# Encoder layer with a mixture of 32 experts: 32 extra rows for each of the 17 largest experts

## The chip, the cores and the metric

The kernel runs on one core of a Trainium2 chip. The metric is the device time of one execution in microseconds (us), taken as the median of several runs. The kernel before takes 2105.02 us (three runs, 2104.12 to 2105.26).

The engines that matter here are TensorE (PE for its products, PEld for its weight loads), VectorE (DVE), ScalarE (ACT), GpSimd (POOL) and the DMA engines, whose large loads are issued from SyncE's queue (SP).

## The reference

One layer over 1024 tokens of width 1024: a mixer (short convolution and Fourier group), a cross attention to 256 memory tokens, and a mixture of experts, which is most of the time:

```
logits = (hf @ w_router) + b_router                 # 1024 tokens, 32 experts
top_v, top_i = top_k(logits, 4)                     # 4 experts for each token
top_w = softmax(top_v)
for each expert e, for the rows (tokens) that chose it:
    gu   = xb @ w_gate_up[e] + b_gate_up[e]         # 1024 -> 2 x 1024
    gate = min(gu[:, :1024], 7); up = clip(gu[:, 1024:], -7, 7)
    out  = ((up + 1) * gate * sigmoid(1.702 * gate)) @ w_down[e] + b_down[e]
y = sum over the four experts of a token of out * weight
```

1024 tokens with four choices each make 4096 rows, 128 for an expert on average. How many rows an expert has depends on the inputs. The reference's inputs are drawn from seed 0 where nothing else is asked.

## The kernel before

Everything is float32. The weights of an expert are 12 chunks of 1 MB (`raw`): eight for gate and up, four for down. A chunk is loaded by SP's queue (line 973), ACT copies it into a rounded part `eh` (line 134), DVE takes the rest `el` (line 135), and PE makes three products for each 128 rows of contraction (lines 1062 to 1064). So a chunk costs PE 12 products, whatever rows the expert really has: the rows are always a block of 128.

The 32 experts are worked through one after another. Expert 0 is a "static" one, handled before the counts are known; the other 31 are sorted by how many rows they have, and the program speaks of ranks: rank 0 is the expert with most rows. Which weights a rank means is read from a table at run time; everything else is fixed when the program is built.

Rows of an expert beyond its first 128 have three ways:

- `rem_rows(r)` gives rank r a fixed number of further rows, 64, 32 or 0. Ranks with some are called heavy here, the others light. For a heavy expert `plan` puts further steps among the steps of the first 128 rows: `x_rem` gathers and transposes the rows (line 1035), six calls of `rem_mm` multiply them by the raw chunks in float32 (line 1085, eight products each, `j` = 1, 3, 5, 7, 9, 11), `take_rem` and `h_rem` make the hidden values (lines 1103 to 1125), and `y_rem` adds the result to memory (lines 1140 to 1145). The first of the six calls and `x_rem` stand in the last chunks of the expert ahead.
- `rem_mm` uses the width of TensorE: with 64 rows two products with different rows of the output run side by side, with 32 rows four do (`n = 64 // m`).
- What no rank's fixed rows hold goes to `beyond`, a loop near the end (line 1402) over blocks of 128 rows, as many as the counts ask for (`nblk`), none if they all fit. `_tables` gives it the room of each rank in `eid[:, 3] = [P + rem_rows(r) for r in e]`.

`rank_order` mixes heavy and light ranks so that they alternate as far as their numbers allow. The kernel before has 18 heavy ranks (two with 64 rows, 16 with 32) and 13 light ones. Its order after the static expert begins with ranks 0, 1, 18, 2, 19, 3, 4, 20, 5, 21, 6, 22, 7, 8. Two heavy experts stand next to each other in five places.

Within an expert, what is done after which half chunk is set by tables of numbers for each kind of expert (`PLACE_*`, `AHEAD_*`, `REM`): they say how many chunks ahead ACT and DVE split. Raw chunks and split pairs share 20 buffers of 8 KB per partition, so a load starts when a buffer comes free. The tables are chosen by kind (heavy, light, first, loop, last) and not by rank. All engines' work is in the order in which the program writes it.

Of the kernel before, what the change touches and what calls it, by code (L numbers as in the profile page):

```python
# [29 lines left out]
ALPHA = 1.702  # L30
N64 = 2
N32 = 18
STATIC = NE - 1
# [46 lines left out]
def kernel(ctx: ExitStack, tc: tile.TileContext, A, out, dbg=None):  # L80
# [39 lines left out]
    def rsqrt(dst, v, tmp):  # L120
        """1 / sqrt of positive columns times RS: a first guess from the exponent, three Newton steps, each without its last factor"""
        nc.vector.tensor_scalar(tmp.bitcast(I32), v.bitcast(I32), 1, None, op0=ALU.logical_shift_right)  # L122
        nc.vector.tensor_scalar(dst.bitcast(I32), tmp.bitcast(I32), -1.0, float(0x5F3759DF), op0=ALU.mult, op1=ALU.add)
        for c in (3.0, 12.0, 768.0):
            if v.shape[-1] == 1:
                nc.vector.scalar_tensor_tensor(tmp, dst, v, dst, op0=ALU.mult, op1=ALU.mult)
            else:
                nc.vector.tensor_tensor(tmp, dst, dst, op=ALU.mult)
                nc.vector.tensor_tensor(tmp, tmp, v, op=ALU.mult)
            nc.vector.scalar_tensor_tensor(dst, tmp, -c, dst, op0=ALU.add, op1=ALU.mult)  # L130
# [20 lines left out]
    def sum_cols(srcs):  # L151
        """sums over the partitions, a token on each partition, 128 tokens for each column; among the products that follow"""
        b = sm_bank("colps")
        k = 0
        for src in srcs:
            for j in range(src.shape[-1] // P):
                def one(k=k, s=src[:, j * P:(j + 1) * P]):
                    nc.tensor.matmul(b[:, k:k + 1], s, ones[:, 0:1], start=True, stop=True)
                fill.append(one)
                k += 1  # L160
        return b[:, :k]

    def rms_cols(b, width, eps_scale=1.0):
        """sums of squares to 1 / rms"""
        while fill:
            fill.pop(0)()
        c = small("rc", [P, 3, 16], bufs=2)
        v, y, t = (c[:, i, :b.shape[-1]] for i in range(3))
        nc.vector.tensor_scalar(v, b, eps_scale / width, eps_scale * EPS, op0=ALU.mult, op1=ALU.add)
        nc.scalar.activation(y, v, AF.Sqrt)  # L170
        nc.vector.reciprocal(y, y)
        nc.vector.tensor_tensor(t, y, y, op=ALU.mult)
        nc.vector.tensor_tensor(t, t, v, op=ALU.mult)
        nc.vector.tensor_scalar(t, t, -0.5, 1.5, op0=ALU.mult, op1=ALU.add)
        nc.vector.tensor_tensor(y, y, t, op=ALU.mult)
        return y
# [8 lines left out]
    def rms_row(dg, dst):  # L185
        """on every partition, a token in each column"""
        ps = sm_bank("rowps")[:, :dg.shape[-1]]
        nc.tensor.matmul(ps, ones, dg, start=True, stop=True)
        nc.scalar.activation(dst, ps, AF.Copy)
# [16 lines left out]

    # weights in their order of use: raw ahead, split one ahead
    specs = [(A["w_in"][12 + c], KT) for c in range(4)]
# [42 lines left out]

    # ---------------------------------------------------------------- constants
    vec = cp.tile([P, 52], F32, name="vec")
# [32 lines left out]

    # ------------------------------------------------------------ x^T and the Fourier group's projection
    xh = [[s8(f"xh{h}{g}", [P, 4, H2], F32R) for g in range(2)] for h in range(2)]
# [73 lines left out]

    # Fourier group: fold over n <-> N - n and n <-> N/2 - n, channel transform
    AB = []
# [43 lines left out]

    # short convolution group
    ych, ycl = [], []  # L410
# [96 lines left out]

    # ------------------------------------------------------------ sequence transform, memory side
    yfh = [s8(f"yfh{q}", [P, 2, S], F32R) for q in range(2)]
# [13 lines left out]
    def seq_out(ct, sb):  # L523
        """in three parts"""
        pq = []
# [80 lines left out]

    # ------------------------------------------------------------ output projection and first residual
    x1h = [[s8(f"x1h{h}{g}", [P, 4, H2], F32R) for g in range(2)] for h in range(2)]
# [39 lines left out]

    # ------------------------------------------------------------ attention over the memory
    # scale of the logits: rms / sqrt(head dim), one column for each token tile  # L650
    sc = []
# [86 lines left out]

    # v W_o for each head, then the second residual
    VW = []  # L740
# [19 lines left out]
    def row_table():  # L760
        """table of expert rows, all padding"""
        ptab = s8("ptab", [P, NE * ESTR // P, 2], I32)
        nc.gpsimd.iota(ptab[:, :, 0], pattern=[[1, NE * ESTR // P]], base=0, channel_multiplier=NE * ESTR // P)
        nc.vector.memset(f(ptab[:, :, 1]), 0.0)
        nc.vector.tensor_scalar(ptab[:, :, 0], ptab[:, :, 0], P - 1, None, op0=ALU.bitwise_and)
        nc.scalar.dma_start(out=tab_d.rearrange("(p j) c -> p j c", p=P), in_=ptab)
# [12 lines left out]
    def load_bias():  # L779
        """leading parts twice, then the rests: products with leading part, rest, leading part of the weights"""  # L780
        bd.extend([s4("bdn", [3 * NE, D], F32R), s4("bdr", [3 * NE, D])])
        for i in range(3):
            nc.scalar.dma_start(out=bd[1][i * NE:(i + 1) * NE], in_=A["b_down"])
# [10 lines left out]

    # ------------------------------------------------------------ router, one tile of 128 tokens at a time
    scat = []
# [4 lines left out]
    def tile_r(x2):  # L801
        """logits of two tiles, an expert on each partition, in four parts"""
        ps = lt["ps"] = sm_bank("lgps")
        for k in range(2):
            for g in range(4):
                nc.tensor.matmul(ps[g * NE:(g + 1) * NE, :HF], wr[:, 2 * g + k, :], x2(2 * g + k), start=k == 0, stop=k == 1)
        sb = lt["sb"] = t2("lgt")[:, :HF]
        nc.scalar.activation(sb, ps[:, :HF], AF.Copy)
# [106 lines left out]

    # ------------------------------------------------------------ experts
    order = rank_order()
# [59 lines left out]
    def whole(q):  # L977
        """chunks that are multiplied in float32 itself, where the tensor engine has the time"""
        return q < WHOLE_FIRST or q >= NE * 12 - WHOLE_LAST
# [90 lines left out]
    def rem_mm(i, j):  # L1070
        """rows 128.. of the pair of chunks j - 1, j: products for different rows of PSUM run side by side"""
        s = st[i]
# [32 lines left out]
    def h_rem(i, c):  # L1105
        """hidden values with the columns on the partitions; each sum has two parts"""
        s = st[i]
# [39 lines left out]
    def expert(i, hook=None, last=False):  # L1147
        """a chunk at a time; what else there is to do has its place after the first half of a chunk or after the chunk"""
        s = st[i]
# [49 lines left out]
    def plan(i):  # L1199
        """rows 128.. of an expert: some chunks ahead of the first 128, so that raw chunks are not held for them"""  # L1200
        lead, lx, lt, l0, l1, ly = REM
# [14 lines left out]

    # ------------------------------------------------------------ second residual, chunk by chunk
    def early():
        """positions of the static expert: rows of the first tiles within its first 128, the others beyond"""
        ps = sm_bank("exps")  # L1220
# [7 lines left out]
    def bias_load():  # L1228
        """gate biases on the first half of the partitions, up biases on the second: a leading part and the rest of each expert"""
        BT.extend([s4("BT", [P, D], F32R), s8("braw", [P, D])])  # L1230
# [26 lines left out]
    def places(*todo):  # L1257
        """what is done after each part of a chunk"""
        return {k: (lambda fs=fs: [fn(*arg) for fn, *arg in fs]) for k, fs in enumerate(todo)}
# [45 lines left out]
    def count_order():  # L1305
# [31 lines left out]
        def surplus():  # L1337
            """blocks of 128 rows beyond the rows that a rank has"""
            ps3[0] = sm_bank("ovps")
# [59 lines left out]
    def beyond():  # L1399
        """rows beyond: any number of blocks of 128"""  # L1400
        ordered.close()
# [52 lines left out]

    # ------------------------------------------------------------ last norm; the last expert's rows once more
    z = NE - 1
# [96 lines left out]
def _cols(w, n):  # L1553
    """[K, F] -> [F / n, P, K / P, n]"""
    return w.reshape(w.shape[0] // P, P, w.shape[1] // n, n).transpose(2, 1, 0, 3)


def _heads(w):
    """[4 * 256, D] -> [head, half of D, P, 2, 512]"""
    return w.reshape(4, 2, P, 2, H2).transpose(0, 3, 2, 1, 4)  # L1560
# [45 lines left out]
```

## Time and profile before

| what | value |
|---|---|
| median of three runs | 2105.02 us |
| span of the profiled execution, first to last instruction | 2097.7 us |
| around the span (median less span) | 7.3 us |
| stages before the experts | 0 to 620.8 us |
| expert 0 (static) | 620.8 to 696.5 us |
| experts 1 to 30 | 696.5 to 2041.0 us |
| last expert and final norm | 2041.0 to 2097.7 us |

The page gives the profiled execution a span and no time of its own; the 7.3 us are the difference from the median of the runs. An expert is taken to begin where PE starts the product with its bias row (line 1049), its first product. In the views below a row of the timeline is start, duration, engine, line, operation, output and inputs; a group row is line, engine, operation, shapes and count, then busy us, mean ns of one, and the engine's idle time before. Matmuls overlap in their durations, so the cost of a step on PE is read from the start of one row to the start of the next. One float32 product stands as two records, and one call of `rem_mm` as a row of x16.

### The profile page before, as it was taken

What the parts mean: (1) busy time and instruction counts of PE and PEld (TensorE: products, weight loads), DVE (VectorE), ACT (ScalarE), POOL (GpSimd) and SP (SyncE); (2) the same over time, 40 slices, a digit from 0 to 9 for tenths busy, and PEclk for the clock granted to TensorE, in tenths of its full rate; (3) what the DMA queues carried; (4) which work ended last, traced back from release to release, by engine and by line L of the source; (5) the groups of instructions that cost most, each with busy time, mean ns of one, the idle gap of its engine ahead of it and who ended that gap; (6) DMA issues with size and microseconds to landing.
All of it is one profiled execution on the core that took longest, in us unless ns stands there. A gap on an engine that the chain in (4) does not pass through costs nothing. (4 is left out here: it accounts for less than half of the span.)

```text
span 2097.7 us, 28863 instructions
## 1 busy us (share of the span) xinstructions
PE 2059.9 (98%) x10857; PEld 1521.2 (73%) x10857; DVE 1590.7 (76%) x2000; ACT 1124.9 (54%) x1200; POOL 233.0 (11%) x192
## 2 busy tenths in 40 slices
PE   8999999999989999999999999999999999999996
PEld 7888988888974567676777676767667767676764
DVE  6666778445666667888888897888888888888886
ACT  5233533344223455676566665667656567566764
POOL 0000100000232111011101011102111101110101
PEclk9999999999999999999999999999999999999998
DMA  4121434013266769897989887988798989798986
GB/s 156 50 65 61 146 120 157 21 41 124 94 245 252 249 224 327 296 327 267 340 309 366 300 318 272 343 304 325 278 331 313 356 296 320 273 344 306 341 303 241
DMA packets 105327, 514.06 MB, mean 245 GB/s; under 512 B 21697, under 2 KB 26050, under 8 KB 56034
## 3 DMA queue, kind: packets, MB, share of 16 engines
q1 hardware_dynamic: 83968, 445.88, 56.3%
q0 software_dynamic: 14400, 49.33, 9.6%
q10 hardware_dynamic: 6818, 16.99, 2.2%
q8 instruction: 86, 1.41, 0.3%
q14 instruction: 55, 0.45, 0.1%
HBM read 473.81 MB, written 38.34 MB: 244 GB/s over the span
## 5 line engine op out<-in xcount | busy, mean ns | idle before, releaser
L135 DVE TENSOR_TENSOR el<-raw,eh 128x2048 fp32r<-128x2048 f32 x372 | 831.3, 2287 | 134.6 <-ACT eh L134 133.1
L134 ACT ACTIVATE eh<-raw 128x2048 fp32r<-128x2048 f32 x372 | 690.5, 1908 | 7.2 <-PEq L1402 4.6
L1062 PE MATMUL g<-eh,xthl 128*128 128x512 f32 x992 | 401.3, 405 | 0.0
L1063 PE MATMUL g<-el,xthl 128*128 128x512 f32 x992 | 388.5, 392 | 2.0 <-DVE el L135 2.0
L1064 PE MATMUL g<-eh,xthl 128*128 128x512 f32 x992 | 388.2, 391 | 2.2 <-issue 2.2
L1062 PEld LDWEIGHTS g<-eh,xthl 128*128 128x128 f32 x992 | 186.5, 188 | 80.8 <-issue 42.6
L1064 PEld LDWEIGHTS g<-eh,xthl 128*128 128x128 f32 x992 | 186.6, 188 | 43.5 <-issue 2.6
L1063 PEld LDWEIGHTS g<-el,xthl 128*128 128x128 f32 x992 | 186.8, 188 | 37.9 <-DVE el L135 2.7
L1062 PE MATMUL d<-eh,hthl 128*128 128x512 f32 x496 | 205.9, 415 | 0.0
L1064 PE MATMUL d<-eh,hthl 128*128 128x512 f32 x496 | 195.0, 393 | 0.0
L1063 PE MATMUL d<-el,hthl 128*128 128x512 f32 x496 | 193.9, 391 | 0.0
L1085 PE MATMUL r<-raw,xrt 128*32 128x512 f32 (+1 forms) x1216 | 166.3, 598 | 0.7 <-ACT xrt L1036 0.7
L1001 ACT ACTIVATE sg<-g 128x512 f32<-128x512 f32 x64 | 40.4, 631 | 171.1 <-DVE g L1000 171.1
L940 POOL DMA_INDIRECT acc_d<-y,idx x31 | 78.2, 2522 | 384.7 <-ACT y L1131 302.4
L1062 PEld LDWEIGHTS d<-eh,hthl 128*128 128x128 f32 x496 | 93.2, 188 | 27.2 <-ACT xthl L134 9.2
L1064 PEld LDWEIGHTS d<-eh,hthl 128*128 128x128 f32 x496 | 93.1, 188 | 21.2
L1063 PEld LDWEIGHTS d<-el,hthl 128*128 128x128 f32 x496 | 93.6, 189 | 16.0
L1085 PEld LDWEIGHTS r<-raw,xrt 128*32 128x32 f32 (+1 forms) x1216 | 39.8, 113 | 87.0 <-issue 85.8
L134 ACT ACTIVATE hthl<-tp 128x512 fp32r<-128x512 f32 x62 | 37.1, 599 | 119.4 <-PE tp L1009 119.4
L145 PE MATMUL mm<-xh,wh 128*128 128x512 f32 x232 | 92.4, 398 | 5.8 <-ACT xh L137 5.8
L147 PE MATMUL mm<-xh,wl 128*128 128x512 f32 x232 | 91.2, 393 | 0.3 <-DVE wl L135 0.3
L146 PE MATMUL mm<-xl,wh 128*128 128x512 f32 x232 | 91.2, 393 | 0.0
(377 smaller groups left out, 3297.7 us busy)
## 6 DMA issues: line engine op xcount, KB each, us to landing
raw<-in_w_exp SPq DMA_DIRECT2D x375, 1024.0 KB
raw<-in_w_exp POOLq DMA_DIRECT2D x9, 1024.0 KB
wraw<-in_w_in SPq DMA_DIRECT2D x15, 512.0 KB
xraw<-in_xT SPq DMA_DIRECT2D x16, 256.0 KB
wraw<-in_w_k SPq DMA_DIRECT2D x8, 512.0 KB
wraw<-in_w_v SPq DMA_DIRECT2D x8, 512.0 KB
wraw<-in_w_out SPq DMA_DIRECT2D x8, 512.0 KB
xres<-in_xT SPq DMA_DIRECT2D x16, 256.0 KB
```

What stands on the lines that cost most here:

```text
L134: nc.scalar.activation(dh, src, AF.Copy)
L135: nc.vector.tensor_tensor(dl, src, f(dh), op=ALU.subtract)
L145: nc.tensor.matmul(ps, lh, rh, start=start and i == 0, stop=False)
L146: nc.tensor.matmul(ps, lh, rl, start=False, stop=False)
L147: nc.tensor.matmul(ps, ll, rh, start=False, stop=stop and i == n - 1)
L940: nc.gpsimd.indirect_dma_start(out=dst, out_offset=bass.IndirectOffsetOnAxis(ap=idx, axis=0), in_=src, in_offset=None, compute_op=ALU.add)
L1001: nc.scalar.activation(sg[:m, :n], g[:m, :n], AF.Sigmoid, scale=ALPHA)
L1062: nc.tensor.matmul(ps, l[:, 0, kk, :], wh[:, k, :], start=j >= 8 and g == 0 and k == 0, stop=False)
L1063: nc.tensor.matmul(ps, l[:, 0, kk, :], wl[:, k, :], start=False, stop=False)
L1064: nc.tensor.matmul(ps, l[:, 1, kk, :], wh[:, k, :], start=False, stop=g == 1 and k == 3)
L1085: nc.tensor.matmul(ps[o:o + m], lhs[:, g * 4 + kk, :], ch[12 * i + j - 1 + t][0][:, kk, :], start=k == 0 and g == 0, stop=k == 4 // n - 1 ...
```

## The change

Two numbers change: no rank has 64 further rows, and 17 ranks instead of 18 have 32.

```
-N64 = 2
-N32 = 18
+N64 = 0
+N32 = 17
 STATIC = NE - 1
```

The other lines of the diff take out comments and docstrings. `rem_rows` thus gives ranks 0 and 1 the number 32, ranks 2 to 16 stay at 32, and rank 17 goes from 32 to 0. The static expert keeps 64. Through `_tables` the loop is told of the smaller room. `rank_order` now has 17 heavy and 14 light ranks: 0, 1, 17, 2, 18, 3, 19, 4, 20, 5, 6, 21, 7, 22. Two heavy ones stand next to each other in three places.

PE at the end of expert 0, just ahead of expert 1's first product (`rd` is a part of expert 0, `r` the first `rem_mm` of expert 1, the two `g` rows its bias):

```order
 L1064 MATMUL d_6126<-eh,hthl 128x512
 L1085 MATMUL rd<-raw,hrt 64x512 x8
-L1085 MATMUL r_6236<-raw,xrt 64x512 x8
+L1085 MATMUL r_6236<-raw,xrt 32x512 x8
 L1049 MATMUL g_6261<-BT,ohr 128x512
 L1049 MATMUL g_6263<-BT,ohr 128x512
```

The number of products stays, eight, and each now makes 32 rows; nothing around them moves.

POOL, from the gathers for expert 5 on (`xg` are the 128 rows of the next expert, `xgr` its further rows, `acc_d<-yr` and `acc_d<-y` the results of the expert that ends); before:

```order
L936 DMA xg<-h_d,idx 128x1024
L936 DMA xgr<-h_d,idr 32x1024
L940 DMA acc_d<-y,idx 1152x1024
L936 DMA xg<-h_d,idx 128x1024
L936 DMA xgr<-h_d,idr 32x1024
L940 DMA acc_d<-yr,ids 2304x512
L940 DMA acc_d<-y,idx 1152x1024
L936 DMA xg<-h_d,idx 128x1024
L940 DMA acc_d<-yr,ids 2304x512
L940 DMA acc_d<-y,idx 1152x1024
```

And now:

```order
L936 DMA xg<-h_d,idx 128x1024
L936 DMA xgr<-h_d,idr 32x1024
L940 DMA acc_d<-y,idx 1152x1024
L936 DMA xg<-h_d,idx 128x1024
L940 DMA acc_d<-yr,ids 2304x512
L940 DMA acc_d<-y,idx 1152x1024
L936 DMA xg<-h_d,idx 128x1024
L936 DMA xgr<-h_d,idr 32x1024
L940 DMA acc_d<-y,idx 1152x1024
```

Where two heavy experts followed each other a light one now stands between them; the same moves are made on PE, DVE and ACT. Taken expert by expert, the rows of PE, DVE and ACT from expert 3 to the end are, in both programs, made of the same few sequences (heavy before light, heavy before heavy, light before heavy, and the last ones); only how often each stands there differs.

## Rows read from the trace of the kernel before

**Rows 1.** The page, part 1: busy time, share of the span, instructions.

```profile
PE 2059.9 (98%) x10857; PEld 1521.2 (73%) x10857; DVE 1590.7 (76%) x2000; ACT 1124.9 (54%) x1200; POOL 233.0 (11%) x192
```

**Rows 2.** Busy time by windows, experts 1 to 30; first its columns.

```profile
core 0: us, PE busy (x) PEld busy (x) DVE busy (x) ACT busy (x) POOL busy (x), PEclk, DMA share, GB/s
696.45:2040.95 1344.50, 1342.35 (x6914) 935.76 (x6912) 1114.54 (x982) 851.70 (x722) 167.10 (x95) 1.00 0.85 310
```

**Rows 3.** Waits of PE from 696 to 2041 us: total, times, longest.

```profile
PE g L1064 <- issue: 2.2, 1, 2.2
```

**Rows 4.** The same view by experts 1, 2, 6, 7, 8 and 30.

```profile
696.45:756.35 59.90, 59.90 (x278) 36.33 (x276) 42.95 (x38) 32.64 (x28) 6.36 (x4) 1.00 0.67 222
756.35:812.04 55.69, 55.69 (x256) 34.71 (x254) 35.12 (x34) 25.47 (x24) 5.71 (x3) 1.00 0.80 280
936.33:985.84 49.51, 49.51 (x280) 32.51 (x276) 40.95 (x41) 31.54 (x28) 6.64 (x4) 1.00 0.70 242
985.84:1032.95 47.11, 47.11 (x256) 31.52 (x252) 36.86 (x37) 27.33 (x25) 7.48 (x3) 1.00 0.94 344
1032.95:1071.55 38.60, 38.60 (x190) 29.72 (x189) 34.47 (x26) 27.20 (x24) 4.69 (x4) 1.00 0.93 347
1991.42:2040.95 49.53, 47.38 (x256) 31.43 (x252) 40.36 (x38) 29.05 (x25) 5.46 (x3) 1.00 0.79 297
```

**Rows 5.** Timeline of PE: one `rem_mm` with 64 rows, one with 32.

```profile
692.91 3.60 PE L1085 MATMUL r<-raw,xrt 128*64 128x512 f32 x16
696.45 0.50 PE L1049 MATMUL g<-BT,ohr 64*128 64x512 f32 x2
...
848.77 1.92 PE L1085 MATMUL r<-raw,xrt 128*32 128x512 f32 x16
850.62 0.50 PE L1049 MATMUL g<-BT,ohr 64*128 64x512 f32 x2
```

**Rows 6.** Timeline of DVE and PE, end of the light experts 8 and 12.

```profile
1063.60 4.50 DVE L135 TENSOR_TENSOR el<-raw,eh 128x2048 fp32r<-128x2048 f32 x2 [1.11 <-ACT eh L134]
...
1067.09 0.39 PE L1063 MATMUL d<-el,hthl 128*128 128x512 f32 x1
...
1235.01 4.50 DVE L135 TENSOR_TENSOR el<-raw,eh 128x2048 fp32r<-128x2048 f32 x2 [1.11 <-ACT eh L134]
...
1238.50 0.39 PE L1063 MATMUL d<-el,hthl 128*128 128x512 f32 x1
```

**Rows 7.** Groups of DVE by shape, experts 1 to 30, further rows only.

```profile
L1116 DVE TENSOR_TENSOR re<-tp,bT 128x256 f32<-128x256 f32 x32 | 13.5, 422 | 8.3 <-PE tp L1113 8.3
L1118 DVE TENSOR_TENSOR re<-re,tp 128x256 f32<-128x256 f32 x32 | 13.5, 421 | 1.1
L1141 DVE TENSOR_TENSOR yr<-rd,yr 64x512 f32<-64x512 f32 x16 | 10.8, 675 | 0.0
L1125 DVE SCALAR_TENSOR_TENSOR hrt<-ga 128x128 f32<-128x128 f32 x32 | 9.4, 294 | 1.1
L1124 DVE TENSOR_TENSOR ga<-ga 128x128 f32<-128x128 f32 x32 | 9.4, 293 | 7.9 <-ACT ga L1122 7.9
L1121 DVE TENSOR_SCALAR ga<-re 128x128 f32<-128x128 f32 x32 | 7.3, 227 | 1.1
L1123 DVE TENSOR_SCALAR ga<-re 128x128 f32<-128x128 f32 x32 | 7.0, 220 | 0.0
```

**Rows 8.** The loop's branches (line 1402), and one chunk multiplied in float32.

```profile
L1402 PEldq COMPARE_BRANCH  x3: 101/187/327, 1997.6 to 2002.0; - x3
...
630.89 3.60 PE L1054 MATMUL g<-raw,xthl 128*128 128x512 f32 x8
```

## The prediction

> **What bounds the kernel now.** I read the page's first part first: PE is busy for 98% of the span [rows 1]. That alone does not prove a bound, since matmul records overlap. So I cut the span into stages and looked at the stretch that the change touches, experts 1 to 30: of 1344.50 us PE has 1342.35 busy, at the granted clock 1.00, its upper level of 2.4 GHz [rows 2], and the waits of PE there are one, of 2.2 us, at the loop [rows 3]. DVE and the DMA engines are well used too (1114.54 us, and a share of 0.85) [rows 2], but PE never waits for them. Then I cut the stretch expert by expert at the bias products. Four kinds of windows come out: heavy before heavy 49.51 us, heavy before light 47.11, light before heavy 38.60, and the two experts with 64 rows, 59.90 and 55.69 [rows 4]. The trace has four windows of the first kind, eleven of the second and twelve of the third, and within a kind they agree to 0.03 us. A window that long and that constant, with PE busy in all of it, is the sum of its products. So time here is the number of PE products times their pace, and what the change does to that number is what it does to the time, as long as the others keep up.
>
> **The price of 32 rows.** Call the work that every expert has b, the part of a heavy expert's further rows that lies in the expert ahead X, and the part in its own window Y. Then b + X + Y = 49.51, b + Y = 47.11 and b + X = 38.60 [rows 4], so X = 49.51 - 47.11 = 2.40, Y = 49.51 - 38.60 = 10.91, b = 36.20. Being heavy with 32 rows costs X + Y = 13.31 us. As a check from below: one `rem_mm` takes from 848.77 to 850.62, 1.85 us [rows 5], and six make 11.1; the other 2.2 us are the small transposes around them.
>
> **The price of 64 rows.** Expert 1 has its own Y64 and expert 2's X64 in its window, expert 2 only its Y64. So Y64 = 55.69 - 36.20 = 19.49, X64 = 59.90 - 55.69 = 4.21, together 23.70 us [rows 4]. Check: one call takes from 692.91 to 696.45, 3.54 us against 1.85 [rows 5], close to double, since two products run side by side instead of four; six calls differ by 10.1 us, and the windows say 23.70 - 13.31 = 10.39.
>
> **What the change does, summed.** Ranks 0 and 1 go from 64 to 32: 2 x 10.39 = 20.8 us of PE. Rank 17 goes from heavy to light: 13.3 us. Together 34.1 us, all of it on PE, where nothing is idle. The order moves too, and this I cost at nothing, since X and Y are paid for each heavy expert wherever it stands. Counted in windows, experts 1 to 30 then have 3 x 49.51 + 14 x 47.11 + 13 x 38.60 + 2.4 for the loop's entry (the last heavy window is 49.53 instead of 47.11 [rows 4]) = 1312.3 against 1344.5 us, 32.2 less, and X64 - X = 1.8 us more goes from the static expert's window: 34.0. The rest of the span, the six last experts with their kinds and the final norm included, has the same work in the same order. Span: 2097.7 - 34.1 = 2063.6 us; with the 7.3 us that the median has beyond the span, **2070.9 us**, 1.6% less.
>
> **What hides what is left.** DVE's and ACT's work per expert hardly changes, but they get 34 us less for it. The cover: in the light-heavy rhythm the last chunk of a light expert is the tightest. In expert 8 the first of two `el` of 4.50 us together ends near 1065.9 and its first product starts at 1067.09, 1.2 us later; two rounds on, in expert 12, near 1237.3 and 1238.50, again 1.2 us [rows 6]. The margin is thin, but it is reset by each heavy expert and doesn't shrink from round to round. The change lengthens the unbroken rounds (the longest from three light experts before the next heavy pair to five), and nothing in the trace drifts with their length. Were that cover gone, a light expert would end later by what DVE lacks. The other place is new: expert 1 with 32 rows straight after the static one. Its window shrinks from 59.90 to 49.51 us with some 42 us of DVE work (42.95 before; 40.95 in another such window) [rows 4]; it fits, with 6.6 us to spare where that other window has 8.6, but the split of its chunks is entered from another state than anywhere in the trace. I bound what that costs between 0 and the 2.0 us by which its slack is smaller. I take 0, since windows with the same rows have no wait.
>
> **A page that says otherwise.** The PE row by itself, 98% [rows 1], is the reason for the sum. The Trainium skill, "Perfetto Trace Analysis", section "Identifying the Most-Contended Engine", holds that matmul busy time doesn't measure how near TensorE is to its limit, and wants the weight loads' share beside it; by that, DVE with 76% stands ahead of PEld with 73% [rows 1], and the change would be worth what it takes from DVE. The rows on PE's waits speak against reading it so here [rows 3]; it is the second rival.
>
> **Rivals.**
>
> *The loop runs (slower).* With zero blocks the loop is some branches: three on PE's queue of at most 0.33 us [rows 8], and no row of its body. The smaller room sends rows there as soon as a rank of 0 or 1 has over 160, or rank 17 over 128; that is the point from which it decides. Routing the reference's inputs of seed 0 through its own router gives ranks 0 to 3 the counts 154, 153, 150, 147, rank 16 130 and rank 17 126. So all fit, with six and two rows to spare, and the loop stays empty. This hangs on the draw: of seeds 1 to 8, seven have one to three ranks over 160. If a block ran, it would cost 12 chunks in float32 at 3.60 us [rows 8], 43 us, were the loads hidden; at 347 GB/s [rows 4] a chunk of 1.05 MB takes 3.0 us, and with loads and products in turn, since a product's two buffers are taken again by the next, 79 us. I take 79, as the loop has nothing else to overlap. 2070.9 + 79 = **2150 us** (2114 at least), and more with more blocks. Against it speak the counts; for it, only that the measured inputs could be drawn otherwise.
>
> *DVE or the loads are the bound (faster, little).* Then only DVE's part goes. A heavy expert has two of each of six groups, 2 x (422 + 421 + 227 + 220 + 293 + 294) ns = 3.75 us, and one of 675 ns [rows 7]: 4.4 us for rank 17, and next to nothing for ranks 0 and 1, which swap wide for narrow ones. 2105.0 - 4.4 = **2100.6 us**, just beyond 0.2%. Against it: PE would have to show waits for DVE now, and has none [rows 3].
>
> *Part of it comes back as stalls.* The thin 1.2 us per light expert [rows 6] turns into a wait, in each of 14 light experts, with at most that size: 2070.9 + 14 x 1.2 = 17 us, **2088 us**; with the 2 us at expert 1 alone, 2073. For it: DVE has 34.47 of 38.60 us in a light window [rows 4]. Against: three rounds in a row are equal to the hundredth.
>
> **How the numbers follow.** The forecast, 2070.9, gets 0.86; stalls that give part back 0.07, DVE as the bound 0.02, the loop 0.04, and 0.01 for a change that does nothing, as when the numbers are not used where I think. From below the bound is the sum itself with 0.03 us on each of 30 windows, some 1 us, the runs' own spread of 1 us, and 1 us for the tail: 2068. From above the 2 us at expert 1 and the runs' 1 us give 2074, and the lower third of the stalls, which lie anywhere between 2071 and 2088, goes to 2077. The range 2068 to 2077 holds the forecast's part and those stalls, some 0.88; the other cases lie outside, and I make it no narrower, as it is only 0.4% wide. A measurement tells about 0.2% (4.2 us) from no change. Faster by more: 0.86 + 0.07 + 0.01 of DVE as the bound = 0.94. Same: 0.02. Slower: 0.04.
>
> **What would show it.** Right: `rem_mm` rows with 64 only in the static expert; windows 1 and 2 of 49.5 and 47.1 us; three windows of 49.5, fourteen of 47.1 (one with the loop), thirteen of 38.6; PE's waits from expert 1 to 30 still about 2.2 us. Wrong: waits of PE for `el` at line 1063, or a light window over 38.7 us (the cover); any row of the loop's body (the counts); windows 1 and 2 longer than said (DVE's reserve after the static expert); or a changed granted clock in the stretch.

## The result

The changed kernel takes 2069.6 us (median of four runs, 2064.7 to 2071.3), the kernel before in the same comparison 2104.6: a ratio of 0.983, 95% interval 0.981 to 0.985. The forecast was 2070.9 us, with 2068 to 2077 as the range. One of the four runs, 2064.7 us, lies below that range.

The page of the changed kernel, part 1 (busy us, share of the span, instructions), answers to [rows 1]:

```profile
PE 2028.4 (98%) x10745; PEld 1513.3 (73%) x10745; DVE 1585.7 (77%) x1991; ACT 1122.3 (54%) x1195; POOL 227.3 (11%) x190
```

PE has 31.5 us less work and its share is still 98%. DVE loses 5.0 us, ACT 2.6. The wide form of `rem_mm` (64 rows) is left with 96 records, which are the six calls of the static expert. By windows, of experts 1 to 30 together and then of experts 1, 2, 3 and 30 (to be read beside [rows 2, 4]):

```profile
core 0: us, PE busy (x) PEld busy (x) DVE busy (x) ACT busy (x) POOL busy (x), PEclk, DMA share, GB/s
698.57:2012.37 1313.80, 1311.64 (x6806) 926.15 (x6802) 1109.37 (x973) 850.42 (x718) 162.16 (x94) 1.00 0.87 317
698.57:748.08 49.51, 49.51 (x282) 32.51 (x278) 40.64 (x40) 32.44 (x29) 8.24 (x5) 1.00 0.73 247
748.08:795.20 47.12, 47.12 (x258) 31.50 (x254) 36.81 (x37) 27.32 (x25) 7.66 (x3) 1.00 0.95 345
795.20:833.80 38.60, 38.60 (x191) 29.73 (x190) 34.51 (x26) 27.21 (x24) 4.80 (x4) 1.00 0.93 346
1961.30:2012.37 51.07, 48.91 (x258) 32.57 (x254) 40.29 (x38) 29.01 (x25) 3.61 (x3) 0.97 0.77 289
```

Expert 1 goes from 59.90 to 49.51 us and expert 2 from 55.69 to 47.12. Cut at the bias products, the trace has three windows of 49.51 or 49.52, thirteen of 47.11 or 47.12, thirteen of 38.59 or 38.60, and the last heavy one with the loop, 51.07. In that last one the granted clock is 0.97 and not 1.00, which is one of the prediction's signs of being wrong; what it cost is said below. PE's waits from 698 to 2012 us, to be read beside [rows 3], are still one:

```profile
PE g L1064 <- issue: 2.2, 1, 2.2
```

The reserve is the time between the end of a split `el` and the start of the product that needs it. Here it is at the end of the first light expert (3) and of the last in the run of five (20), timeline of DVE and PE as in [rows 6]:

```profile
825.81 4.50 DVE L135 TENSOR_TENSOR el<-raw,eh 128x2048 fp32r<-128x2048 f32 x2 [1.11 <-ACT eh L134]
...
829.30 0.39 PE L1063 MATMUL d<-el,hthl 128*128 128x512 f32 x1
...
1560.98 4.49 DVE L135 TENSOR_TENSOR el<-raw,eh 128x2048 fp32r<-128x2048 f32 x2 [1.11 <-ACT eh L134]
...
1564.47 0.39 PE L1063 MATMUL d<-el,hthl 128*128 128x512 f32 x1
```

The first of the two `el` ends near 828.1 and 1563.2, its first product starts at 829.30 and 1564.47: 1.2 us, as before. Five rounds in a row did not wear it down. Nothing of the loop's body is in the trace: the counts fit.

### The profile page after: what moved, and what is told of

Its sections match the earlier page's. It is cut to its first block, busy times and chain, and to the rows that moved or that the text cites. A ratio compares the mean times of both kernels' runs of the same rounds, so it can differ in the third digit from the quotient of the medians.

```text
span 2067.6 us, 28604 instructions
## 1 busy us (share of the span) xinstructions
PE 2028.4 (98%) x10745; PEld 1513.3 (73%) x10745; DVE 1585.7 (77%) x1991; ACT 1122.3 (54%) x1195; POOL 227.3 (11%) x190
## 5 line engine op out<-in xcount | busy, mean ns | idle before, releaser
L1085 PE MATMUL r<-raw,xrt 128*32 128x512 f32 (+1 forms) x1152 | 144.8, 598 | 0.7 <-ACT xrt L1036 0.7
L135 DVE TENSOR_TENSOR wl<-wraw,wh 128x1024 fp32r<-128x1024 f32 (+1 forms) x57 | 70.3, 1233 | 22.9 <-ACT wh L134 18.9
```

What stands on the lines that cost most here:

```text
L135: nc.vector.tensor_tensor(dl, src, f(dh), op=ALU.subtract)
L1085: nc.tensor.matmul(ps[o:o + m], lhs[:, g * 4 + kk, :], ch[12 * i + j - 1 + t][0][:, kk, :], start=k == 0 and g == 0, stop=k == 4 // n - 1 ...
```

## The experiments

The kernels of this section were measured in three further comparisons. The kernel before was in each of them and took 2100.4 to 2101.6 us (medians); the ratios are to that. All diffs are against the changed kernel.

### The two parts apart

only_64_to_32:

```
 N64 = 0
-N32 = 17
+N32 = 18
```

> Only the first part of the change: ranks 0 and 1 get 32 rows instead of 64, rank 17 stays heavy (0 and 18 instead of 2 and 18). If time is the sum of PE's products: 2 x 10.39 = 20.8 us less than before, 2084 us beside 2104.6; expert windows 49.5 and 47.1 us for experts 1 and 2, all others as before. If DVE were the bound: no difference, since wide groups take the place of narrow ones, 2104 to 2105.

only_17_light:

```
-N64 = 0
+N64 = 2
 N32 = 17
```

> Only the second part: rank 17 loses its 32 rows, ranks 0 and 1 keep 64 (2 and 17). By the sum: 13.3 us less than before, 2091 us; one heavy window fewer, light windows still 38.6. If DVE were the bound: 4.4 us less, 2100. If the parts were not additive, the two savings would not give the 34 of the whole change.

Measured: ranks 0 and 1 alone, 2081.3 us, ratio 0.990 (0.987 to 0.993), some 21 us less; rank 17 alone, 2086.0 us, 0.993 (0.991 to 0.995), some 15 us less. The product of the two ratios is 0.983, the ratio of the whole change. The windows say it more exactly; of only_64_to_32 experts 1 and 2, and of only_17_light experts 1 to 3 and then 1 to 30 together:

```profile
695.59:745.11 49.52, 49.52 (x280) 32.51 (x276) 40.57 (x40) 32.45 (x29) 8.47 (x5) 1.00 0.74 248
745.11:792.22 47.11, 47.11 (x256) 31.51 (x252) 36.90 (x37) 27.33 (x25) 6.08 (x3) 1.00 0.92 342
```

```profile
697.04:756.94 59.90, 59.90 (x280) 36.33 (x278) 42.78 (x38) 32.64 (x28) 6.55 (x4) 1.00 0.66 223
756.94:812.63 55.69, 55.69 (x256) 34.72 (x254) 35.12 (x34) 25.47 (x24) 5.83 (x3) 1.00 0.78 279
812.63:851.21 38.58, 38.58 (x191) 29.72 (x190) 34.20 (x26) 26.78 (x23) 8.29 (x4) 1.00 0.92 346
697.04:2029.81 1332.77, 1330.61 (x6804) 933.19 (x6802) 1109.60 (x967) 848.07 (x715) 151.47 (x93) 1.00 0.86 312
```

In only_17_light experts 1 to 30 take 1332.77 us instead of 1344.50; the last of them is 1.5 us longer as in the changed kernel, so the part is worth 13.3. In only_64_to_32 experts 1 and 2 together are 19.0 us shorter, and by the prediction's X64 - X another 1.8 belong to the window of the static expert, in whose last chunks expert 1's further rows begin: 20.8. That window as a whole can't show the 1.8, since its length with 32 rows differs by 1.3 us between the traces (73.4 to 74.7 us); the one `rem_mm` in it takes 1.86 us instead of 3.54. DVE as the bound would have given nothing for the first part, as DVE's work in the two windows falls by 0.6 us only, and the loads as the bound nothing for either, as every expert loads its 12 chunks as before. The first part gave the larger saving.

### More of it

```
-N64 = 0
-N32 = 17
+N64 = 4
+N32 = 18
```

> The dose turned up: ranks 2 and 3 get 64 rows too (4 and 18). By the sum: 2 x 10.39 = 20.8 us more than before, 2125 us. If idle time or the loads hide part of a wide expert's products where it stands between light ones: less than 20.8. DVE as the bound: no difference.

Measured: 2120.9 us, ratio 1.0095 (1.007 to 1.012), some 20 us more. Experts 3 to 6 of this kernel (light, heavy with 64 rows, light, heavy with 64 rows before a heavy one; before they were 38.59, 47.11, 38.59 and 49.51):

```profile
812.41:852.77 40.36, 40.36 (x189) 30.38 (x188) 35.32 (x27) 28.73 (x24) 7.47 (x4) 1.00 0.92 335
852.77:908.46 55.69, 55.69 (x254) 34.71 (x252) 38.08 (x35) 27.27 (x24) 2.56 (x2) 1.00 0.74 258
908.46:948.82 40.36, 40.36 (x189) 30.37 (x188) 35.32 (x27) 28.73 (x24) 7.55 (x4) 1.00 0.91 334
948.82:1007.01 58.19, 58.19 (x278) 35.70 (x276) 40.23 (x37) 29.39 (x26) 3.46 (x3) 1.00 0.62 208
```

They add up to 20.8 us more: the price of 64 instead of 32 rows is the same between light experts as it was at the start.

### The order

```
-        order.append(light.pop(0) if (i + 1) * nl // n > i * nl // n else heavy.pop(0))
+        order.append(heavy.pop(0) if heavy else light.pop(0))
```

> The changed kernel with another order: all 17 heavy ranks first, then the 14 light ones, everything else as it is. The prediction cost the order at nothing. By the sum alone: 2070 us, with heavy windows of 49.5 and light ones of 36.2. If the alternation is what gives DVE and the loads their time: a light expert followed by a light one has 36.2 us of PE, and DVE's 34.5 us with its waits no longer fits, so PE waits for el there, up to some 3 us in each of 13 windows, 2075 to 2110 us.

> The grouped order without the loop; rows beyond the fixed room would be left out, of which these inputs have none. It tells what of the 13 us of the grouped order is the order and what is the loop standing in a light expert. In grouped_order PE waited 0.75 us for hh in eleven light windows, and the last window before the end took 50.6 us. If the rest is the loop's entry: the last window falls to 36.8, and the time is 2062.6 (no_loop) + 12 x 0.75 = 2072. If the light experts themselves end later one after another: above 2075.

Measured: 2083.4 us, ratio 0.990 (0.988 to 0.993), and without the loop (with the edit of no_loop, below, on top of this one) 2077.0, 0.9885 (0.987 to 0.9905). So the order is not free as such. Of grouped_order the first light window, the next two, and the last before the end:

```profile
1539.53:1575.43 35.90, 35.90 (x167) 28.81 (x165) 32.02 (x24) 25.08 (x21) 3.83 (x2) 1.00 1.00 382
1575.43:1612.19 36.76, 36.05 (x167) 28.75 (x165) 34.44 (x25) 26.33 (x21) 3.90 (x2) 1.00 0.93 352
1612.19:1648.94 36.75, 36.06 (x167) 28.73 (x165) 34.47 (x26) 26.36 (x21) 4.36 (x2) 1.00 0.96 368
1979.30:2029.94 50.64, 39.64 (x165) 30.97 (x164) 39.44 (x27) 29.89 (x22) 3.90 (x2) 0.90 0.80 302
```

and PE's waits from 699 to 2030 us:

```profile
PE tp L1009 <- DVE hh L1004: 7.6, 11, 0.8
PE g L1049 <- issue: 5.2, 1, 5.2
PE d L1064 <- DVE hthl L135: 3.3, 1, 3.3
PE d L1062 <- ACT hthl L134: 2.5, 1, 2.5
```

A light expert between a heavy and a light one needs 35.9 us, and not the 36.2 that the prediction's equations gave for b: X, Y and b add up only to within 0.3 us. From the second on, PE waits 0.7 us in a light expert, but not for `el` as I expected: for `hh`, the hidden values, which DVE makes between two `el`. The rest of the loss is in the last window, where a light expert stands at the loop's place. Without the loop that window still took 42.4 us and not the 36.8 I expected: PE waited 1.0 us and 3.3 us for `hthl` (the hidden values, transposed and split), and then the clock was granted at half for 3.4 us, 1.7 us lost. That the tables of the loop's place don't suit a light expert is a guess; no run tests it. So half of my expectation for the second kernel was right (the loop is part of it, 50.6 against 42.4 us) and half was not.

### The reserve

```
         todo[h1].append(lambda: h_main(i, 1))
+        if not m:
+            def idle_work():
+                for _ in range(6):                 # 1, 4 or 6
+                    nc.vector.tensor_reduce(dum, ones[:, None, :].to_broadcast([P, 4, P]), axis=AX.X, op=ALU.add)
+            todo[h1].append(idle_work)
...
+    dum = small("dum", [P, 4])
```

> The changed kernel with one more DVE reduction (128x512, some 0.68 us, its result unused) in each light expert, just ahead of the two el whose first product follows 1.2 us after. DVE waits 1.1 us for ACT there, so the reduction goes into that wait: no difference, light windows 38.6, 2070 us. If DVE were the bound: 14 x 0.68 = 9.5 us more, 2079.

> The same with six reductions, some 4.1 us, in each light expert. By the margins read from the timeline: 4.1 - 1.1 (DVE's wait for ACT) - 1.2 (reserve at the first product) = 1.8 us of wait of PE for el in each of 13 light windows, 23 us more, 2093 us; light windows 40.4. If DVE were the bound: 57 us more, 2127. If the reserve is larger than read: no difference.

> As dve_six_more, with four reductions in each light expert. Six took 4.19 us of DVE and made a light window 1.96 longer. If the reserve is a threshold of 1.1 + 1.2 us as read from the timeline: 4 x 0.70 - 2.35 = 0.45 us of wait, light windows of 39.0 to 39.2, 6 us more than the changed kernel. If a light window grew in proportion to what DVE is given: 38.6 + 4/6 x 1.96 = 39.9, 17 us more.

Measured: with one reduction 2070.3 us (0.985, 0.983 to 0.987), no clear difference from the changed kernel's 0.983; with four 2083.6 (0.992, 0.990 to 0.994); with six 2100.9 (1.0006, 0.9995 to 1.0017). Expert 3, a light one, with one, four and six:

```profile
794.80:833.39 38.59, 38.59 (x191) 29.71 (x190) 35.06 (x27) 27.18 (x24) 4.45 (x4) 1.00 0.95 353
```

```profile
791.74:830.86 39.12, 38.88 (x189) 29.71 (x188) 35.95 (x30) 27.42 (x24) 5.07 (x4) 1.00 0.93 340
```

```profile
791.60:832.16 40.56, 38.88 (x189) 29.72 (x188) 37.32 (x32) 27.42 (x24) 7.01 (x4) 1.00 0.91 336
```

PE's waits with four (695 to 2022 us) and with six (695 to 2040 us):

```profile
PE g L1062 <- issue: 7.4, 1, 7.4
PE d L1063 <- DVE el L135: 3.2, 13, 0.2
```

```profile
PE d L1063 <- DVE el L135: 21.9, 13, 1.7
PE g L1062 <- issue: 7.7, 1, 7.7
```

The light windows are longer by nothing, 0.5 us and 2.0 us for 0.7, 2.8 and 4.2 us of work: a threshold at 2.3 us, not a proportion. (The list of waits has 0.25 of the 0.5 us and 1.7 of the 2.0; the other 0.3 us of each stands as busy time of PE, 38.88 against 38.59.) The 1.1 us that DVE waits for ACT and the 1.2 us ahead of the product are what [rows 6] showed, and the thirteen waits are at the product and the place named. The total with four came near the 17 us of the other theory, but for another reason: 13 x 0.52 = 6.8 us stand in the light windows, and 6.5 in the last heavy one (57.5 against 51.07 us), where entering the loop now holds PE for 7.4 instead of 2.2 us.

### The loop

loop_one_block:

```
-N32 = 17
+N32 = 16
```

> The changed kernel with 16 instead of 17 heavy ranks: rank 16, which has 130 rows, loses its 32, so two rows go to the loop, which runs one block. By the sum its light expert saves 13.3 us and the block costs between 43 us (products alone) and 79 us (loads and products in turn): 2100 to 2136 us, 2136 taken. If the block hides behind the experts' work, 2057; if it costs more than loads and products in turn, above 2136.

no_loop, where the chunks also keep the two buffers that were set aside for the loop:

```
-            slots[0] = SLOTS - 2
-        expert(i, {BEYOND: beyond} if i == NE - 2 else None)
+            slots[0] = SLOTS
+        expert(i)
```

> The changed kernel without the loop; rows beyond the fixed room would be left out, of which these inputs have none. The empty loop's price: PE waits 2.2 us at its branches and its clock falls for 3.4 us after it, 1.7 us lost, so 2.2 to 4 us less, 2066 us, and a last heavy window of 47.1 instead of 51.1. If the wait is hidden by something else that is late, no difference.

Measured with one block: 2124.2 us, ratio 1.0116 (1.010 to 1.013). Two rows too many turn a gain of 1.7% into a loss of 1.2%. The window with the loop, and PE's waits from 1945 to 2065 us:

```profile
1945.56:2065.53 119.97, 102.64 (x376) 54.88 (x372) 45.82 (x46) 34.05 (x33) 6.86 (x5) 0.91 0.65 236
```

```profile
PE g L1064 <- issue: 8.5, 1, 8.5
PE tp L1415 <- DMA oxg<-h_d,idx: 4.3, 1, 4.3
PE mm L1431 <- DMA oraw<-in_w_exp: 2.3, 4, 1.5
```

119.97 less 51.07 is 68.9 us for a block, inside my bounds of 43 and 79 but not at the end that I took. Loads and products do not take turns: PE waits 2.3 us for raw chunks in all. The block is 43 us of products, the way in and out (PE waits 4.3 us for the rows and 8.5 us at the end), the bias products, and a clock that was granted at half twice, for 10.2 us at its start (from 1957.5 us) and for 10.2 us from 2019.0 us on, of which PE spent the first 5.9 us in the wait at the end.

Without the loop: 2062.6 us, 0.9825 (0.981 to 0.984). Its last heavy window:

```profile
1957.82:2004.90 47.08, 47.08 (x256) 31.52 (x252) 40.20 (x38) 29.02 (x25) 3.62 (x3) 1.00 0.86 312
```

That is 47.08 us instead of 51.07, so the empty loop costs 4.0 us in the changed kernel's trace: the wait of 2.2 us and 1.7 us for the clock at half. In the kernel before, where the clock did not fall there, it cost 2.4 us (49.53 against 47.11). The total is 3 us below the expected 2066, for a reason that is not the loop: in this trace the experts begin at 620.4 us, in the changed kernel's at 625.2 (why, below). It is the fastest kernel here, but it would lose rows for inputs that fill an expert further, so it is a measure of the loop and not a replacement.

## Why the prediction held, and where it didn't

**The sum.** It forecast 32.2 us less for experts 1 to 30. Measured are 1344.50 - 1313.80 = 30.7, and the last heavy window is 1.5 us longer for a reason outside the sum: after the loop's wait the clock was granted at half for 3.4 us in the changed kernel and not before. Without that it is 32.2. The 1.5 us came back behind the experts, where the sum has no change. The last expert and the final norm, before and after:

```profile
2040.95:2097.70 56.75, 40.43 (x141) 25.92 (x140) 35.18 (x58) 25.36 (x35) 8.80 (x6) 0.87 0.66 244
2012.37:2067.60 55.23, 38.40 (x141) 24.90 (x140) 35.28 (x58) 25.52 (x35) 9.20 (x6) 0.91 0.67 250
```

In the kernel before, the clock was at half for 3.4 us there, from 2062.5 us on, just after PE had waited 1.7 us for `el`; the changed kernel has no such stretch at that place. Each term was tested by itself: 10.39 us for 64 instead of 32 rows by only_64_to_32 and more_64, 13.3 for being heavy by only_17_light.

**The order costs nothing.** True of this order, as the windows show, but I argued it too widely ("paid for each heavy expert wherever it stands"). With light experts in a row PE waits 0.7 us in each for `hh`. The alternation is part of the cover.

**The cover.** The 1.2 us and DVE's wait of 1.1 us before it were read rightly, and expert 1 after the static one, which I had bounded with 0 to 2 us, cost nothing: 49.51 us. The price of the stalls rival had no ground: it took the reserve of 1.2 us as the most that a wait can be, and six reductions made a light window 2.0 us longer.

**The rule on the most contended engine.** By the weight loads' share, which the Trainium skill ("Perfetto Trace Analysis", section "Identifying the Most-Contended Engine") wants, beside the share of peak operations (MFU), in place of the matmul row, DVE stood ahead of PE. The prediction left that second measure out. only_64_to_32 decides: it takes next to nothing from DVE and gave 21 us. Here the measurement goes with the matmul row, since the row came with another sign, a single wait of 2.2 us on PE in 1344 us. The rival's title named the loads too, but the prediction gave them no price; they would have meant no change at all, since no bytes of the weights go away, and the same run rules them out.

**The loop.** The rival's condition was exact (two rows decide), its price was 79 us where 68.9 were measured: I took the end of the bounds at which nothing overlaps, and loads do run ahead.

**Steps that were wrong without showing.** I took the 7.3 us between the median and the profiled span as time around the span. The runs of the changed kernel list both: 2069.46 us with a span of 2067.6, 1.9 us around it. So the profiled execution of before took some 2099.6 us (an estimate, 2097.7 + 1.9), and the other 5 us belonged to executions that differ from it. Their cause shows in the windows of the changed kernel and of before, 365 to 375 us, in a stage that the change does not touch:

```profile
365.00:375.00 10.00, 10.00 (x49) 10.00 (x48) 5.24 (x7) 2.74 (x4) 0.00 (x0) 0.50 0.28 96
```

```profile
365.00:375.00 10.00, 10.00 (x69) 9.28 (x70) 7.80 (x14) 4.50 (x7) 0.00 (x0) 1.00 0.43 142
```

The granted clock is 0.50, the level of 1.2 GHz, for 10.2 us in one and 1.00 in the other. The program is the same there; at half the clock fewer of its products fit into ten us (49 records against 69). The experts begin at 625.2 us in the changed kernel and at 620.8 in the one before. My span of 2063.6 us was measured as 2067.6: 4.4 us more ahead of the experts, 1.5 more at the loop, 1.5 less behind the experts and 0.5 less in the static expert's window; a run of the changed kernel with a mean clock of 0.997 instead of 0.994 had 2062.8. That the time came within 1.3 us all the same is partly luck: the three runs of before that I started from were among its long ones (all its runs in this study lie between 2097.9 and 2106.5 us) and three of the four runs of the changed kernel are long too (spans of 2067.6, 2069.4 and 2067.7 us). That these other runs owe it to the same stretch is inferred, as they left no trace: in the other comparisons the runs of before above 2104 us have mean clocks of 0.992 to 0.994, those below 2099 us 0.995 to 0.997. For the same reason the 1 us that the range gave to the spread of the runs was too small; the four runs of the changed kernel lie 6.6 us apart.

## What to carry to other kernels

Where an engine's busy share is near the whole span, cut the stretch into repeating units, and see whether the units are equal to the hundredth and that engine hardly ever waits: then a change is the sum of what it takes from that engine, and differences of unit lengths give the price of a step more fully than its main instructions do (13.3 us here, where six calls of `rem_mm` make 11.1). Read the reserve of the second engine at its tightest place before trusting the sum, with the idle time ahead of it counted in; a threshold is what decides, and reordering can use it up. And where fixed room is cut to the data, the price of one row too many (here 69 us for a block against 13 us saved) says how sure of the data one has to be.

## What the runs showed of the hardware

The granted clock of TensorE fell after waits that are the same in all executions, and not in each of them. Ahead of the stretch at 365 us PE waited 1.0 and 0.8 us for its weights; all twelve traces of this study have these waits, and three have the fall: grouped_order, dve_one_more and the changed kernel (10.2, 6.8 and 10.2 us at 1.2 GHz). After the loop's wait of 2.1 or 2.2 us the clock fell for 3.4 us in the changed kernel, only_64_to_32, only_17_light and dve_one_more (last heavy windows of 51.06 to 51.09 us), and not in the kernel before and more_64 (49.53 and 49.45). What decides stays open.

Entering a loop with no turns costs 4.0 us with that fall of the clock and 2.4 us without it. It costs more when a scatter lands late. SP's queue waits at the loop for the last scatter-add, first in the changed kernel and then with six reductions, where PE's wait there is 7.7 instead of 2.2 us:

```profile
SPq L1402 <- DMA acc_d<-y,idx: 4.6, 1, 4.6
```

```profile
SPq L1408 <- DMA acc_d<-y,idx: 16.9, 2, 15.5
```

Three single windows were long for once. In only_64_to_32 (39.76 us) and dve_one_more (42.37) PE waited 1.1 and 2.1 us for a gather of further rows (`xgr`), and in the second of them the clock was then granted at half for 3.4 us. In grouped_no_loop (37.81) it waited 0.9 us for a gather of the first 128 rows (`xg`). The lists of PE's waits of the other traces have nothing of the kind in experts 1 to 30 (loop_one_block has it for the rows of its block).
